# Token scales moved from x to the projections, and x laid out transposed, in a hybrid attention and Hyena encoder layer on one Trainium2 core

## The chip, the cores and the metric

The kernel runs on one core of one Trainium2 chip, as one launch. The metric is the device time in microseconds; the time before is the median of three runs, 1343.47 us (1342.41 to 1346.18). The profile below is of one further execution, of 1344.2 us from its first to its last instruction. Engines are named as in the profile: PE does matmuls (PEld: its weight loads), DVE, ACT and POOL do elementwise work, SP issues most transfers.

## What is computed

One encoder layer is applied to two sequences of 512 tokens by 1024 channels, all in float32. The layer norms x, projects it, sends a third of the projected columns each way through dilated attention (q, k, v) and Hyena (u), and ends with an output projection and an MLP. What the change touches is the beginning:

```
def rmsnorm(x, g):
    y = x * rsqrt(mean(x * x, axis=-1) + EPS) * g
...
xn = rmsnorm(x, mix_norm)
proj = xn @ w_in                      # 1024 -> 512 q, 512 k, 512 v, 1536 u
q = rope(rmsnorm_f32(q, q_norm))      # per head of 64
k = rope(rmsnorm_f32(k, k_norm))
attn = dilated_attention(q, k, v)
hy = hyena_mixer(u, ...)              # width-3 conv along tokens, then two gated long convolutions
h = x + concat(rmsnorm(attn), rmsnorm(hy)) @ w_out
y = h + square(relu(rmsnorm(h) @ w_up)) @ w_down
```

The norm of x has one factor for each token and one for each channel. The projection sums over channels, so the token's factor can be applied before it or after it.

## The kernel before

Every float32 product is formed of three matmuls on operands split in a high and a low part (mm3, line 75): high by high, high by low, low by high. Operands are named so: xh and xl are x normed, transposed to [channel, token] and split, one pair of tiles for each sequence with eight blocks of 128 channels; whi and wlo are weights; ih and il, yh and yl are inputs of the transforms.

**Ahead of the projections.** x is loaded as [token, channel], four tiles of 128 tokens for each sequence (load_x, line 138). norm_x (line 161) sums the squares of each tile (half on DVE, half on ACT), takes the power -1/2 on POOL, scales the tile in place (x<-x,ssx), and then, channel block by channel block, turns the four tiles on PE into a bank (pst<-ident,x, line 178), from which ACT makes xh with the channel's gain and DVE makes xl. The gains come as rows of a parameter tile that PE turns into columns (line 151). norm_x of the first sequence runs before all else; that of the second is a stream among others.

**The projections.** proj_u (line 372) does quarter q of u: for each sequence and each of three parts a, 24 matmuls of 128x512 into a bank psu of two; ACT and DVE then form the width-3 convolution y from the bank (one ACT pass, two DVE passes), PE turns y (pst<-ident,y), ACT copies it out as ut, and SP stores it (u_d). proj_qkv forms q, k and v in banks psq of two, 48 matmuls of 128x256 each; for q and k the sum of squares of each head goes through DVE and POOL to a power, and rotary tables ab, made on POOL by rope_tables, are multiplied in; v is copied out by one ACT pass of a bank.

**Beside them.** The Hyena filters (hidden, filters) and then the Hyena units (hyena(q, o), for four quarters and two orders) run transforms: psf forward, psi inverse, each of four classes of 12 matmuls. A class runs psf, then products on DVE (t), a split (yh, yl), then psi. Behind the last projection come the attention and the output projection; the MLP follows as further phases.

**What sets the order.** The work up to the MLP is written as generators, which interleave (line 489) calls by turns: each yields what PE and DVE time it believes it has emitted, and the stream whose work should be ready, by priority, goes next. The streams are: norm_x of the second sequence, then tables, hidden, filters of the four quarters; two streams of Hyena units that begin when the filters are done; one stream of U0 to U3, the Q projections and the attention; and the output projection. What is written this way is then scheduled when the program is built, and each engine executes its list in order: an instruction that waits holds all behind it on that engine. Transfers wait in the same way on SP's queue.

Of the kernel before, what the change touches and what calls it, by code (L numbers as in the profile page):

```python
# [24 lines left out]
# ring sizes  # L25
# [30 lines left out]
def hybrid_encoder_kernel(ctx: ExitStack, tc: tile.TileContext, i: dict, outs, dbg=None):  # L56
# [8 lines left out]
    # ---------------------------------------------------------------- helpers  # L65
# [9 lines left out]
    def mm3(ps, pairs, start=True, stop=True):  # L75
        """ps += sum of products of split operands (w_hi, w_lo, x_hi, x_lo)."""
        n = 3 * len(pairs)
        k = 0
        for wh, wl, xh, xl in pairs:
            for w, x in ((wh, xh), (wh, xl), (wl, xh)):  # L80
                nc.tensor.matmul(ps, lhsT=w, rhs=x, start=start and k == 0, stop=stop and k == n - 1)  # L81
                k += 1
# [24 lines left out]
    ssx = cp.tile([128, 8], F32, name="ssx")  # L107
    ssh = cp.tile([128, 8, 4], F32, name="ssh")
# [3 lines left out]
    # banks of the attention, while the hyena's are in use  # L112
# [3 lines left out]
    def rstd(out, ss, n):  # L116
        """out = (ss / n + eps) ** -0.5 for a few columns."""
# [4 lines left out]
    # ================================================================ phase A  # L122
# [13 lines left out]
    xs = {}  # L136

    def load_x(s, queue=nc.sync, pin=lambda x: x):
        for t in range(4):
            if s == 0 or t == 0:  # L140
                xs[s, t] = rz.tile([128, D], F32, name="x", tag="z", bufs=ZB)
            else:
                xs[s, t] = re_.tile([128, D], F32, name="x", tag="g", bufs=3)
            pin(queue.dma_start(xs[s, t], x_in[s][t * 128:(t + 1) * 128]))
# [4 lines left out]
    nc.sync.dma_start(i2, i["c_i2"])  # L149
    ps0 = bank("ps0", "tr")  # L150
    nc.tensor.transpose(ps0[:, :128], prm, ident)
    nc.vector.tensor_copy(cols, ps0[:, :80])
# [8 lines left out]
    def norm_x(s):  # L161
        for t in range(4):
            x = xs[s, t]
            c = slice(4 * s + t, 4 * s + t + 1)
            junk = [lw.tile([128, 512], F32, name="junk", tag=("y", "ut")[k], bufs=2) for k in range(2)]
            lo, hi = x[:, :512], x[:, 512:]
            nc.vector.tensor_tensor_reduce(out=junk[0], in0=lo, in1=lo, scale=1.0, scalar=0.0,
                                           op0=ALU.mult, op1=ALU.add, accum_out=rsc[:, 0, c])
            act(junk[1], hi, AF.Square, accum_out=rsc[:, 1, c])
            tt(nc.vector, ssx[:, c], rsc[:, 0, c], rsc[:, 1, c], ALU.add)  # L170
            rstd(ssx[:, c], ssx[:, c], D)
            act(hi, hi, AF.Copy, scale=ssx[:, c])
            nc.vector.tensor_scalar(lo, lo, ssx[:, c], None, op0=ALU.mult)
            yield 0, 1.2, 0
        for d in range(8):
            ps = bank("pst", "hx")
            for t in range(4):
                nc.tensor.transpose(ps[:, t * 128:(t + 1) * 128], xs[s, t][:, d * 128:(d + 1) * 128], ident)
# [1238 lines left out]
```

## Time and profile before

| | |
|---|---|
| median of three runs | 1343.47 us (1342.41 to 1346.18) |
| the profiled execution, its span | 1344.2 us |
| instructions | 19082 |
| POOL | busy 145.1 us, 11% of the span, 121 instructions |
| DMA | 184.46 MB, mean 137 GB/s |

The span in 40 equal slices of 33.6 us, each digit the busy share of a slice in tenths; PEclk is the clock granted to PE:

```
PE   6999999999999999999999999999999999999998
DVE  6887658888887755656557998788776688678885
ACT  6434424664565564557547643433333654334350
PEclk9999999999999989999999999999999999999999
```

Slice 1 holds the loading and scaling of x; slices 2 to 6 the u projections and filters; slices 7 to 13 the Q projections and Hyena units; slices 14 to 20 the attention and the output projection; the rest is the MLP. PE is the engine that fills the span, so the time is PE's matmuls plus what PE waits, plus what it loses at a lower clock. An instruction of the profile is given as line, engine, operation, output<-inputs; a wait is put down to the engine and tile that released it.

### The profile page before, as it was taken

What the parts mean: (1) busy time and instruction counts of PE and PEld (TensorE: products, weight loads), DVE (VectorE), ACT (ScalarE), POOL (GpSimd) and SP (SyncE); (2) the same over time, 40 slices, a digit from 0 to 9 for tenths busy, and PEclk for the clock granted to TensorE, in tenths of its full rate; (3) what the DMA queues carried; (4) which work ended last, traced back from release to release, by engine and by line L of the source; (5) the groups of instructions that cost most, each with busy time, mean ns of one, the idle gap of its engine ahead of it and who ended that gap; (6) DMA issues with size and microseconds to landing.
All of it is one profiled execution on the core that took longest, in us unless ns stands there. A gap on an engine that the chain in (4) does not pass through costs nothing.

```text
span 1344.2 us, 19082 instructions
## 1 busy us (share of the span) xinstructions
PE 1312.8 (98%) x6933; PEld 1097.1 (82%) x6933; DVE 1000.6 (74%) x1579; ACT 647.2 (48%) x1463; POOL 145.1 (11%) x121
## 2 busy tenths in 40 slices
PE   6999999999999999999999999999999999999998
PEld 5788889999999767776787788888887888887887
DVE  6887658888887755656558997788776688678885
ACT  6434424664565564557547643433333654334350
POOL 1100001343343030021004000000000000001000
PEclk9999999999999989999999999999999999999999
DMA  7535324224331573232141454544428753463323
GB/s 248 188 114 165 120 93 135 78 67 139 113 92 49 149 241 107 88 112 102 48 135 38 157 189 140 162 152 154 142 104 313 279 167 126 157 235 109 94 64 125
DMA packets 137235, 184.46 MB, mean 137 GB/s; under 512 B 9580, under 2 KB 77076, under 8 KB 137141
## 3 DMA queue, kind: packets, MB, share of 16 engines
q1 hardware_dynamic: 135700, 176.70, 40.7%
q0 software_dynamic: 864, 4.46, 0.9%
q10 hardware_dynamic: 576, 2.10, 0.4%
q8 instruction: 54, 0.88, 0.3%
q14 instruction: 41, 0.33, 0.1%
HBM read 122.66 MB, written 60.56 MB: 136 GB/s over the span
## 4 chain that ended last, share of the span: by engine, by line
PE 85%; DVE 8%; ACT 3%; DMA 2%; issue 2%; POOL 1%; SPq 0%; DVEq 0%; ACTq 0%
PE pu L81 24%; PE pn L81 19%; PE psu L81 10%; PE psq L81 6%; PE psw L81 6%; PE psf L81 4%; PE pss L81 4%; PE psi L81 3%; PE psp L813 2%; PE pv L820 1%; PE pv L819 1%; DVE clo L70 1%; PE po L832 1%; PE pst L372 1%; DVE t L70 1%
## 5 line engine op out<-in xcount | busy, mean ns | idle before, releaser
L81 PE MATMUL pu<-hn,chl 128*128 128x512 f32 x768 | 184.9, 390 | 1.9 <-POOL hn L70 1.9
L81 PEld LDWEIGHTS pu<-hn,chl 128*128 128x128 f32 x768 | 144.1, 188 | 32.4 <-POOL hn L70 2.7
L81 PE MATMUL pn<-hn,chl 128*128 128x512 f32 x576 | 141.5, 392 | 2.0 <-ACT chl L67 1.7
L81 PEld LDWEIGHTS pn<-hn,chl 128*128 128x128 f32 x576 | 108.7, 189 | 26.1 <-ACT chl L67 2.6
L67 ACT ACTIVATE chi<-fa 128x1024 fp32r<-128x1024 f32 x49 | 51.9, 1060 | 124.5 <-PE pu L81 63.1
L81 PE MATMUL psq<-wlo,xh 128*128 128x256 f32 x384 | 108.8, 283 | 0.4 <-DVE wlo L70 0.4
L81 PE MATMUL psq<-whi,xl 128*128 128x256 f32 x384 | 108.7, 283 | 0.0
L81 PE MATMUL psq<-whi,xh 128*128 128x256 f32 x384 | 108.6, 283 | 0.0
L70 DVE TENSOR_TENSOR clo<-fa,chi 128x1024 fp32r<-128x1024 f32 x49 | 61.3, 1251 | 39.4 <-ACT chi L67 39.4
L81 PE MATMUL pu<-chi 128*128 128x512 f32 x248 | 86.5, 397 | 2.0 <-DVE chi L70 1.1
L81 PE MATMUL pu<-clo,chi 128*128 128x512 f32 x200 | 78.2, 391 | 1.6 <-DVE clo L70 1.6
L81 PE MATMUL pn<-chi 128*128 128x512 f32 x228 | 79.1, 389 | 0.0
L67 ACT ACTIVATE chl<-tmp 128x512 fp32r<-128x512 f32 x64 | 40.3, 631 | 79.7 <-PE pu L81 49.1
L81 PE MATMUL psu<-xh,whi 128*128 128x512 f32 x192 | 77.9, 409 | 0.5 <-ACT xh L67 0.5
L81 PE MATMUL pu<-chi,clo 128*128 128x512 f32 x200 | 77.8, 389 | 0.0
L81 PE MATMUL psu<-xl,whi 128*128 128x512 f32 x192 | 76.9, 401 | 0.0
L81 PE MATMUL psf<-ih,dft 128*128 128x256 f32 x384 | 76.7, 283 | 0.0
L81 PE MATMUL psu<-xh,wlo 128*128 128x512 f32 x192 | 76.2, 398 | 0.0
L81 PE MATMUL pn<-clo,chi 128*128 128x512 f32 x192 | 74.9, 390 | 0.1
L81 PE MATMUL pn<-chi,clo 128*128 128x512 f32 x192 | 74.7, 389 | 0.0
L81 PEld LDWEIGHTS psq<-wlo,xh 128*128 128x128 f32 x384 | 73.7, 192 | 0.6 <-DVE wlo L70 0.6
L81 PEld LDWEIGHTS psq<-whi,xh 128*128 128x128 f32 x384 | 73.7, 192 | 0.0
(246 smaller groups left out, 3240.1 us busy)
## 6 DMA issues: line engine op xcount, KB each, us to landing
fa<-f_d SPq DMA_DIRECT2D x49, 512.0 KB, 3.7
wur<-in_w_up_t_dram SPq DMA_DIRECT2D x32, 512.0 KB, 4.2
f_d<-x SPq DMA_DIRECT2D x60, 256.0 KB, 2.8
wd<-in_w_down_dram SPq DMA_DIRECT2D x14, 1024.0 KB, 7.7
f_d<-s SPq DMA_DIRECT2D x45, 256.0 KB, 2.1
wraw<-in_w_u_dram SPq DMA_DIRECT2D x24, 256.0 KB, 2.9
u_d<-ut SPq DMA_DIRECT2D x24, 256.0 KB, 2.5
z<-u_d SPq DMA_DIRECT2D x24, 256.0 KB, 4.1
```

What stands on the lines that cost most here:

```text
L67: nc.scalar.activation(out, in_, func, **kw)
L70: eng.tensor_tensor(out, a, b, op=op)
L81: nc.tensor.matmul(ps, lhsT=w, rhs=x, start=start and k == 0, stop=stop and k == n - 1)
L372: nc.tensor.transpose(pt[:, t], y[:, t * 128:(t + 1) * 128], ident)
L813: nc.tensor.transpose(ps[:, t * 128:(t + 1) * 128], exps[n][1 + t][:, kt * 128:(kt + 1) * 128], ident)
L819: nc.tensor.matmul(pv, lhsT=w, rhs=ph, start=kt == 0, stop=False)
L820: nc.tensor.matmul(pv, lhsT=w, rhs=pl, start=False, stop=kt == 3)
L832: nc.tensor.matmul(po[:, t], lhsT=ot[:, t * 128:(t + 1) * 128], rhs=i2, start=True, stop=True)
```

## The change

The host lays x out a second time, as [sequence, pair of channel blocks, channel, block, token], and the parameters as columns, so that neither is turned on PE. xh and xl are then made from the loaded block directly, with the channel's gain and without the token's factor. The squares of a block are summed over blocks by ACT and POOL; PE sums them over channels by products with a column of ones and spreads the resulting factors over the partitions by four plain f32 products with the identity (token_scales); ACT copies them out as the tile scales.

The token's factor is applied behind the projections: to u's bank by one DVE product before the convolution; to v by ACT's copy, now one for each half bank; for q and k, whose heads are normed anyway, only the epsilon changes (epsx), by two operations in place of one. The copy of x that is added to the output is loaded as before.

The first pass, that of the first quarter of u for the first sequence, is written block by block: each channel block goes into three banks at once as it arrives, and the three banks wait for the scales. The rotary tables share their memory with scales and are made behind the last u projection. In the diff, blank lines and comments are left out:

```diff
-    nc.sync.dma_start(ident, i["c_ident"])
...
-    prm = re_.tile([128, 128], F32, name="prm", tag="t", bufs=TB)
-    nc.sync.dma_start(prm, i["params"])
-    load_x(0)
-    nc.tensor.transpose(ps0[:, :128], prm, ident)
-    nc.vector.tensor_copy(cols, ps0[:, :80])
+    pin(nc.sync.dma_start(cols, i["params"]))
...
+    scales = lw.tile([128, NSEQ, 512], F32, name="scales", tag="ab")
+    def load_x(s, j):
+        if s == 0 or j == 0:
+            xr[s, j] = rz.tile([128, 2, 512], F32, name="x", tag="z", bufs=ZB)
+        else:
+            xr[s, j] = re_.tile([128, 2, 512], F32, name="x", tag="g", bufs=3)
+        pin(nc.sync.dma_start(xr[s, j], i["x_t"][s, j]))
+    def prep_x(s, d):
+        x = xr[s, d // 2][:, d % 2]
+        act(xh[s][:, d], x, AF.Copy, scale=col(R_MIX + d))
+        stt(xl[s][:, d], x, col(R_MIX + d), f32(xh[s][:, d]), ALU.mult, ALU.subtract)
+        sq = re_.tile([128, 512], F32, name="sqx", tag="t", bufs=TB)
+        act(sq, x, AF.Square)
+        if d == 0:
+            ssum[s] = sq
+        else:
+            tt(nc.gpsimd, ssum[s], ssum[s], sq, ALU.add)
+    def token_scales(s):
+        c = slice(4 * s, 4 * s + 4)
+        ps = bank("pst", "hx", [128, 4])
+        for t in range(4):
+            nc.tensor.matmul(ps[:, t:t + 1], lhsT=ssum[s][:, t * 128:(t + 1) * 128], rhs=one, start=True, stop=True)
+        marks = [nc.vector.tensor_scalar(rsc[:, 0, c], ps, 1.0 / D, EPS, op0=ALU.mult, op1=ALU.add),
+                 nc.gpsimd.tensor_tensor(ssx[:, c], rsc[:, 0, c], mhalf[:, :4], op=ALU.pow)]
+        nc.vector.tensor_scalar(epsx[:, c], rsc[:, 0, c], EPS, None, op0=ALU.mult)
+        ps = bank("pst", "hx")
+        for t in range(4):
+            nc.tensor.matmul(ps[:, t * 128:(t + 1) * 128], lhsT=ssx[:, 4 * s + t:4 * s + t + 1].to_broadcast([128, 128]),
+                             rhs=ident, start=True, stop=True)
+        return [m.ins for m in (*marks, nc.scalar.activation(scales[:, s], ps, AF.Copy))]
+    def norm_x(s, marks):
         for d in range(8):
-            ps = bank("pst", "hx")
-            for t in range(4):
-                nc.tensor.transpose(ps[:, t * 128:(t + 1) * 128], xs[s, t][:, d * 128:(d + 1) * 128], ident)
-            act(xh[s][:, d], ps, AF.Copy, scale=col(R_MIX + d))
-            stt(xl[s][:, d], ps, col(R_MIX + d), f32(xh[s][:, d]), ALU.mult, ALU.subtract)
-            yield 0.43, 0.66, 0
+            with tc.issue_after(marks[0]), tc.issue_after(marks[1]), tc.issue_after(marks[2]):
+                prep_x(s, d)
+            yield 0, 0.8, 0
+        token_scales(s)
+        yield 1.2, 1.2, 1.0
...
     def proj_u(q, w=None, begun=()):
...
+                if s == 0 and begun:
+                    ps = begun[a]
+                    if a > 1:
+                        turn(*todo.pop(0))
+                        yield 0.43, 0, 0
...
+                tt(nc.vector, ps, ps, scales[:, s], ALU.mult)
                 y = lw.tile([128, 512], F32, name="y", tag="y", bufs=2)
                 act(y, ps, AF.Identity, scale=col(R_CW + 12 + ch), bias=col(R_CB + ch))
...
             if which == 2:
-                act(o, ps)
+                for a in range(2):
+                    act(o[:, a], ps[:, a], AF.Copy, scale=ssx[:, 2 * mp + a:2 * mp + a + 1])
...
-            rstd(rr, rr, HD)
+            for a in range(2):
+                nc.vector.tensor_scalar(rr[:, 4 * a:4 * a + 4], rr[:, 4 * a:4 * a + 4], 1.0 / HD,
+                                        epsx[:, 2 * mp + a:2 * mp + a + 1], op0=ALU.mult, op1=ALU.add)
+            tt(nc.gpsimd, rr, rr, mhalf[:, :8], ALU.pow)
...
-    w0 = load_w(w_u[0], first=True)
+    w_raw = []
+    for j in range(4):
+        load_x(0, j)
+        for k in ((0, 1), (2,), (3, 4), (5,))[j]:
+            w_raw.append(lw.tile([128, 512], F32, name="wraw", tag="wraw", bufs=4) if k < 4 else
+                         re_.tile([128, 512], F32, name="wraw", tag="t", bufs=TB))
+            pin(nc.sync.dma_start(w_raw[k], w_u[0][:, k]))
+    pin(nc.sync.dma_start(ident, i["c_ident"]))
+    for j in range(4):
+        load_x(1, j)
+    w0, begun = [], [bank("psu", tag) for tag in ("mm", "mm", "hx")]
+    for j in range(4):
+        prep_x(0, 2 * j)
+        w0 += load_w(w_u[0], ((0, 1), (2,), (3, 4), (5,))[j], first=True)
+        prep_x(0, 2 * j + 1)
+        for e in (2 * j, 2 * j + 1):
+            for a in range(3):
+                mm3(begun[a], [(*u_unit(w0, e, a), xh[0][:, e], xl[0][:, e])], start=e == 0, stop=e == 7)
+    marks = token_scales(0)
...
-        rope_tables()
...
-        stream(("x1", (), norm_x(1)), ("t", (), tables()), ("h", (), hidden()), ("F0", (), filter0()),
+        stream(("x1", (), norm_x(1, marks)), ("t", (), tables()), ("h", (), hidden()), ("F0", (), filter0()),
...
-        stream(*[(f"U{q}", (), proj_u(q, w0 if q == 0 else None)) for q in range(4)],
+        stream(*[(f"U{q}", (), proj_u(q, *((w0, begun) if q == 0 else ()))) for q in range(4)],
+               ("T", (), rope_tables()),
```

Three places show how the engines' lists change. The first is PE's list at the end of the first pass, in before the last transposes of x (pst<-ident,x) of the first 72 psu matmuls; xh_117 and xl_119 belong to the first sequence there, and so do xh_106 and xl_108 in the changed kernel, where xh_107 and xl_109 are the second's:

```order
51 L178 MATMUL pst<-ident,x 128x128 x4
52 L81 MATMUL psu<-xh_117,wlo 128x512
53 L178 MATMUL pst<-ident,x 128x128 x8
54 L372 MATMUL pst<-ident,y 128x128 x4
55 L81 MATMUL psu<-xh_117,whi 128x512
56 L81 MATMUL psu<-xl_119,whi 128x512
```

```order
64 L81 MATMUL psu<-xl_108,whi 128x512
65 L81 MATMUL psu<-xh_106,wlo 128x512
66 L173 MATMUL pst<-one,sqx 128x1 x4
67 L179 MATMUL pst<-ident,ssx 128x128 x4
68 L386 MATMUL pst<-ident,y 128x128 x4
69 L81 MATMUL psu<-xh_107,whi 128x512
```

The transposes of x are gone. In their place all 72 matmuls of the first pass stand ahead of the sums over channels (row 66), the spreading of the scales (67) and the turning of the first y (68), and no matmul of the second sequence stands before row 69.

The second place is DVE's list at the same point. In before, the first y stands among the second sequence's xl:

```order
46 L70 TENSOR_TENSOR ssx<-rsc 128x1 x2
47 L119 TENSOR_SCALAR ssx<-ssx 128x1 x2
48 L173 TENSOR_SCALAR x<-x,ssx 128x512 x2
49 L73 SCALAR_TENSOR_TENSOR y<-psu,cols,y 128x511 x3
50 L73 SCALAR_TENSOR_TENSOR xl_120<-pst,cols,xh_118 128x512
51 L73 SCALAR_TENSOR_TENSOR y<-psu,cols,y 128x511
52 L73 SCALAR_TENSOR_TENSOR xl_120<-pst,cols,xh_118 128x512 x7
```

```order
10 L70 TENSOR_TENSOR wlo<-wraw,whi 128x512
11 L174 TENSOR_SCALAR rsc<-pst 128x4
12 L176 TENSOR_SCALAR epsx<-rsc 128x4
13 L70 TENSOR_TENSOR psu<-psu,scales 128x512 x3
14 L73 SCALAR_TENSOR_TENSOR xl_109<-x,cols,xh_107 128x512 x8
15 L73 SCALAR_TENSOR_TENSOR y<-psu,cols,y 128x511 x6
```

Now the three banks are scaled first, then all eight xl of the second sequence are made, and only then the first y. ACT's list has the same order: the copy of the scales, then eight xh and six squares of the second sequence, then the first y. The first entry of ACT's list, its table load, which waits for nothing in before, now carries the wait for the first block of x.

The third place is ACT's list at the end of the projections, from the copies of v's last banks (qo<-psq) on; ih and yh are the splits of a Hyena class ahead of its psf and of its psi, v<-vin is the attention's reload of v:

```order
251 L67 ACTIVATE ih<-sd 128x512
252 L67 ACTIVATE ih<-craw 128x512 x2
253 L67 ACTIVATE qo<-psq 128x512
254 L67 ACTIVATE yh<-t_4593 128x512
255 L67 ACTIVATE wsb<-psi 128x512
256 L67 ACTIVATE qo<-psq 128x512
257 L67 ACTIVATE yh<-t_4698 128x512
258 L67 ACTIVATE yh<-t_4839 128x512
259 L67 ACTIVATE wsb<-psi 128x512
260 L67 ACTIVATE qkh<-psk 128x512 x2
261 L67 ACTIVATE v_5461<-vin 128x8x64
262 L67 ACTIVATE yh<-t_4900 128x512
```

```order
251 L67 ACTIVATE qo<-psq,ssx 128x256 x2
252 L67 ACTIVATE ih<-sd 128x512 x2
253 L67 ACTIVATE ih<-craw 128x512
254 L67 ACTIVATE v_5431<-vin 128x8x64
255 L67 ACTIVATE ih<-craw 128x512
256 L67 ACTIVATE yh<-t_4465 128x512
257 L67 ACTIVATE v_5440<-vin 128x8x64
258 L67 ACTIVATE qkh<-psk 128x512 x2
259 L67 ACTIVATE wsb<-psi 128x512
260 L67 ACTIVATE qkh<-psk 128x512 x2
261 L67 ACT_TABLE_LOAD
262 L67 ACTIVATE pe,den<-pe,mx 128x512
```

Behind the last copy of v stood three yh of the last Hyena unit; now all four ih of it stand there too, with the reload of v ahead of the last one.

More of the change, by code (lines that the diff above doesn't have):

```diff
@@ L102, in hybrid_encoder_kernel @@
     ident = cp.tile([128, 128], F32, name="ident")
-    nc.sync.dma_start(ident, i["c_ident"])
+    one = cp.tile([128, 1], F32, name="one")
+    nc.vector.memset(one, 1.0)
     mhalf = cp.tile([128, 16], F32, name="mhalf")
@@ L107, in hybrid_encoder_kernel @@
     ssx = cp.tile([128, 8], F32, name="ssx")
+    epsx = cp.tile([128, 8], F32, name="epsx")
     ssh = cp.tile([128, 8, 4], F32, name="ssh")
@@ L159, in hybrid_encoder_kernel @@
     xl = [la.tile([128, 8, S], F32R, name=f"xl{s}") for s in range(NSEQ)]
-    def norm_x(s):
-        for t in range(4):
[L163 to L174, printed above, removed]
-        for d in range(8):
-            ps = bank("pst", "hx")
-            for t in range(4):
-                nc.tensor.transpose(ps[:, t * 128:(t + 1) * 128], xs[s, t][:, d * 128:(d + 1) * 128], ident)
-            act(xh[s][:, d], ps, AF.Copy, scale=col(R_MIX + d))
-            stt(xl[s][:, d], ps, col(R_MIX + d), f32(xh[s][:, d]), ALU.mult, ALU.subtract)
-            if s == 0 and d == 3:
-                load_x(1, nc.scalar, tc.keep_in_program_order)
-            yield 0.43, 0.66, 0
@@ L191, in load_w @@
             lo = lw.tile([128, 512], F32R, name="wlo", tag="wlo", bufs=WB)
-            raw = (re_.tile([128, 512], F32, name="wraw", tag="t", bufs=TB) if first and k > 1 else
-                   lw.tile([128, 512], F32, name="wraw", tag="wraw", bufs=4))
-            nc.sync.dma_start(raw, src[:, k])
+            if first:
+                raw = w_raw[k]
+            else:
+                raw = lw.tile([128, 512], F32, name="wraw", tag="wraw", bufs=4)
+                nc.sync.dma_start(raw, src[:, k])
@@ L385, in proj_u @@
                 ch = 4 * a + q
-                ps = bank("psu", "mm")
-                for d in range(0, 8, 2):
-                    mm3(ps, [(*unit(e, a), xh[s][:, e], xl[s][:, e]) for e in (d, d + 1)], start=d == 0, stop=d == 6)
-                    yield 1.28, 0, 0
-                    if d == 2 and todo:
-                        turn(*todo.pop())
-                        yield 0.43, 0, 0
+                if s == 0 and begun:
+                    ps = begun[a]
+                    if a > 1:
+                        turn(*todo.pop(0))
+                        yield 0.43, 0, 0
+                else:
+                    ps = bank("psu", "mm")
+                    for d in range(0, 8, 2):
+                        mm3(ps, [(*u_unit(w, e, a), xh[s][:, e], xl[s][:, e]) for e in (d, d + 1)], start=d == 0, stop=d == 6)
+                        yield 1.28, 0, 0
+                        if d == 2:
+                            while todo:
+                                turn(*todo.pop(0))
+                                yield 0.43, 0, 0
+                tt(nc.vector, ps, ps, scales[:, s], ALU.mult)
                 y = lw.tile([128, 512], F32, name="y", tag="y", bufs=2)
@@ L507, in interleave @@
                 break
+    ab = None
     def rope_tables():
+        nonlocal ab
+        ab = lw.tile([128, 4, 4, 64], F32, name="ab", tag="ab")
         cs = lw.tile([128, 4, 2, 32], F32, name="cs", tag="y", bufs=2)
@@ L594, in filter0 @@
         yield from filters(0)
-    for _ in norm_x(0):
-        pass
     done.add("x0")
```

38 lines of the change are left out of this document (17 added, 21 removed).

## The prediction

> **What bounds the kernel now.** The profiled execution lasted 1344.2 us from its first to its last instruction; the median of the three timed runs is 1343.47 us. I make the sum against 1344.2 and read the result as a median, since the two differ by less than 0.1%. First the table of engines, then the waits of PE (columns: us in total, times, longest):
>
> ```profile
> PE 1312.8 (98%) x6933; PEld 1097.1 (82%) x6933; DVE 1000.6 (74%) x1579; ACT 647.2 (48%) x1463; POOL 145.1 (11%) x121
> ...
> PE pst L178 <- DVE x L173: 6.6, 4, 4.3
> ```
>
> PE is busy 98% of the span, and its longest wait by total, 6.6 of the 31.4 us that are left, is for x to be scaled in the first 15 us. So only three things can move the end: matmuls that go or come, the first microseconds, and new idle time of PE. Now the timeline of PE (start, length), and its totals in some stretches (length, then busy us and count, granted clock behind them):
>
> ```profile
> 15.29 1.22 PE L81 MATMUL psu<-xh,whi 128*128 128x512 f32 x2 [0.51 <-ACT xh L67]
> ...
> 18.01 0.63 PE L81 MATMUL psu<-xh,whi 128*128 128x512 f32 x1
> 18.44 0.63 PE L81 MATMUL psu<-xl,whi 128*128 128x512 f32 x1
> ...
> 21.42 0.39 PE L81 MATMUL psu<-xl,whi 128*128 128x512 f32 x1
> 21.65 0.40 PE L81 MATMUL psu<-xh,wlo 128*128 128x512 f32 x1
> ...
> 39.67 1.04 PE L178 MATMUL pst<-ident,x 128*128 128x128 f32 x8
> ...
> 41.01 0.48 PE L81 MATMUL psu<-xl,whi 128*128 128x512 f32 x1
> ...
> 15.29:41.01 25.72, 20.54 (x70) 13.90 (x71) 2.90 (x4) 1.56 (x2) 1.00 0.75 270
> ...
> 475.00:480.00 5.00, 2.87 (x21) 1.00 1.06 339
> 480.00:482.00 2.00, 1.17 (x9) 1.00 1.06 373
> ...
> 482.20:492.40 10.20, 10.20 (x33) 0.50 0.74 258
> ...
> 738.00:741.60 3.60, 1.60 (x5) 1.00 0.00 0
> 741.60:745.00 3.40, 3.40 (x9) 0.50 0.15 11
> ```
>
> Projection work starts at 15.29. A 128x512 matmul follows the last after 0.43 us until 21.4 us and after 0.23 us from then on: half clock for 6.1 us. By 41.01 us, 70 of the first sequence's 72 are done (the row 15.29:41.01 counts psu alone; PEld and the other engines follow PE in it), and all 64 transposes of x lie before that point, 0.11 us each at full clock (eight in 1.04 with the last one's tail), with two turned y. The other rows show what a pause costs: 2.96 us of idle PE between 475 and 482 us, then half clock to about 492 us though PE is busy throughout; 2.0 us of idle before 741.6, then half clock for 3.4 us.
>
> **The change, part by part.** *The first pass starts earlier.* Rows of ACT and SP:
>
> ```profile
> 0.72 1.28 ACT L67 ACT_TABLE_LOAD   x1 [0.72 <-PEq L1406]
> 1.64 1.86 SPq L144 DMA_DIRECT2D x<-in_x_prompt_dram  x4
> 5.48 0.63 ACT L67 ACTIVATE junk<-x 128x512 f32<-128x512 f32 x1 [3.47 <-DMA x<-in_x_prompt_dram]
> 6.82 0.63 ACT L67 ACTIVATE junk<-x 128x512 f32<-128x512 f32 x1 [0.62 <-DMA x<-in_x_prompt_dram]
> ...
> 11.88 1.13 ACT L67 ACTIVATE whi<-wraw 128x512 fp32r<-128x512 f32 x2
> 28.15 1.34 ACT L67 ACTIVATE x<-x,ssx 128x512 f32<-128x512 f32 x2 [1.39 <-POOL ssx L70]
> ```
>
> The first block of x is now second on SP's queue, not third, so it lands about 0.5 us earlier, at 5.0. ACT's table load, which ran at 0.72 us under cover, now holds the wait for that block: 1.28 us more, 6.3. Two xh (0.67 each, as x<-x,ssx) and a whi (0.57): first matmul at 8.2, against 15.29. The rest of x and w (3.0 MB) lands by 13, at 1.34 us for 512 KB (5.48 to 6.82). ACT's 8 xh, 6 whi and 8 squares take 8 x 0.67 + 14 x 0.57 = 13.3 us, to 19.6, well ahead of PE. With 6.1 us at half clock as before (14 matmuls) and 58 x 0.23 = 13.3, the 72 end at 27.6.
>
> *But then PE waits.* By the order, it next forms the sums of squares, spreads the scales, and turns the first y before the second sequence's first matmul:
>
> ```profile
> L70 POOL TENSOR_TENSOR rsc<-rsc,mhalf 128x4 f32<-128x4 f32 x2 | 2.0, 1006 | 85.6 <-DVE rsc L119 85.6
> ...
> L230 PE MATMUL psh<-ft,wr 33*128 33x512 f32 x4 | 2.2, 641 | 0.0
> L70 DVE TENSOR_TENSOR t<-psf,hs 128x512 f32<-128x512 f32 x64 | 40.7, 682 | 8.5 <-PE psf L81 5.1 <-issue 2.1 <-POOL il L70 1.2
> L67 ACT ACTIVATE ut<-pst 128x512 f32<-128x512 f32 x24 | 14.2, 593 | 4.9 <-PE pst L372 4.7
> L67 ACT ACTIVATE y<-psu,cols 128x512 f32<-128x512 f32 x24 | 18.7, 778 | 62.3 <-PE psu L81 55.8 <-POOL ab L70 6.5
> L119 DVE TENSOR_SCALAR rr<-rr 128x8 f32<-128x8 f32 x16 | 2.7, 170 | 8.2 <-ACT sq L67 8.2
> ...
> 31.71 2.19 DVE L73 SCALAR_TENSOR_TENSOR y<-psu,cols,y 128x511 f32<-128x511 f32 x3 [2.51 <-ACT y L67]
> 33.39 0.63 PE L372 MATMUL pst<-ident,y 128*128 128x128 f32 x4 [0.41 <-DVE y L73]
> ```
>
> Plain f32 products occur in before at 512 columns, four records in 2.2 us for two: 1.1 each, so 0.27 for 128 columns; a single column is bounded by 0 and 0.27, and I take 0.2, as its weights still have to be loaded. The wait: 0.8 (four single columns), 0.17 (DVE), 1.0 (POOL's power of 128x4), 1.1 (four spreads), 0.6 (ACT's copy): scales at 31.3. Only then does ACT take up the second sequence, and its 8 xh and 6 squares stand ahead of the first y: 8 x 0.67 + 6 x 0.57 = 8.8, then 0.8 for y and three DVE passes of 0.73: 43.1. DVE's scaling of the three banks (as t<-psf,hs, a product of a bank and a tile: 0.68 each) and its eight xl run beside ACT. With the turn (0.63) the second sequence starts at 43.7. Before, two matmuls were missing at 41.01: 41.5. That is 2.2 us late, and one turn (4 x 0.11) is still owed: **+2.6**. PE has then been idle for 12 us in one piece, so it restarts at half clock. By the rows above that lasts 3.4 to 10.2 us and costs 0.47 us for each (0.43 against 0.23 a matmul): 1.6 to 4.8. I take 5.1 us, between the 3.4 and the start's 6.1: **+2.4**. The second sequence's scales cost PE 0.8 + 1.1 = **+1.9**, their wait covered by projections. In all **+7**; with a denser start and a short ramp it is +3, with a long one +10.
>
> The Trainium skill, in "TensorE: Matmul & The Clock Gate", section "Why this matters for your kernels", speaks against the change here: a pause of more than about 3 us between bursts of matmuls puts the clock back to half. The trace agrees, and shows it for 2.0 us of idle too (738 to 741.6). By the page's Part 1 one busy window of about 3.4 us lifts the clock again, which would make my 2.4 an estimated 1.6; the trace at 482 to 492 shows three times that, 4.8.
>
> *Scaling in the banks.* 24 DVE passes of 0.68 = 16 us come into a stretch that PE bounds and DVE nearly fills:
>
> ```profile
> 40.00:50.00 10.00, 10.00 (x47) 6.78 (x45) 8.36 (x12) 3.40 (x7) 5.22 (x10) 1.00 0.40 113
> 50.00:60.00 10.00, 10.00 (x45) 7.41 (x44) 9.13 (x16) 6.12 (x10) 0.00 (x0) 1.00 0.32 91
> 60.00:80.00 20.00, 20.00 (x92) 15.81 (x91) 18.02 (x35) 7.95 (x13) 0.00 (x0) 1.00 0.54 158
> ```
>
> Behind the length stand PE, PEld, DVE, ACT and POOL: DVE is busy 9.13 of 10 and 18.02 of 20. Three or four more passes in 20 us put it over 100%. PE has projections of later quarters to go on with, so I price the direct wait at 0 to 4, **+2**. What suffers is the filters, which slide behind the projections. The second tensor_scalar per bank of q and k (0.17 on DVE) and v's second copy (at most the 0.59 of ut on ACT) come where these engines have slack. The rotary tables now stand behind the last U; POOL's ten operations are the 5.2 us in the fifth place of 40 to 50. Against them stands PE's rate late among the Q matmuls:
>
> ```profile
> 430.00:440.00 10.00, 10.00 (x86) 1.00 0.09 28
> ```
>
> 86 matmuls in 10.0 us, 0.12 each: two banks of Q (96 matmuls, 11.5 us) hide the 5.2; uncovered they would cost all of it.
>
> *The far end of the projections.* Before the first Q matmul PE's order holds 240 psf matmuls in before and 192 now; behind the last one it holds 12 psf and 36 psi in before, 48 and 48 now: a whole Hyena unit of four classes instead of the end of one. Rows of that place (first and last start), and of the engines that feed a class:
>
> ```profile
> L81 PE MATMUL psq<-whi,xl x38: 279/283/283, 424.8 to 443.9; 128*128 128x256 f32 x38
> ...
> L81 PE MATMUL psi<-yh,dft x31: 279/283/562, 440.4 to 458.1; 128*128 128x256 f32 x31
> ...
> 440.00:460.00 20.00, 17.59 (x111) 0.91 0.77 193
> 460.00:480.00 20.00, 16.93 (x81) 1.00 0.64 190
> ...
> L70 DVE TENSOR_TENSOR t<-t,t 128x256 f32<-128x256 f32 x64 | 32.1, 548 | 0.2
> L70 DVE TENSOR_TENSOR yl<-t,yh 128x512 fp32r<-128x512 f32 x32 | 26.5, 839 | 5.8 <-ACT yh L67 5.5
> L67 ACT ACTIVATE yh<-t 128x512 fp32r<-128x512 f32 x32 | 20.2, 632 | 17.0 <-DVE t L70 16.2 <-DVE rr L119 0.7
> ```
>
> The 48 left over took 14.2 us (443.9 to 458.1) in a stretch where PE was idle 2.4 of 20 us and lost a tenth of its clock. The order puts 36 psf and 12 psi more there. A class runs in turn: 12 matmuls (1.4), four DVE passes (2 x 0.68 + 2 x 0.55), yh 0.63, yl 0.84, 12 matmuls (1.4): 6.7 us. Three more with nothing beside them: 20; less the 5.8 us that PE works on 48 matmuls, 14 of idle and half clock; if attention's first heads fill it all, 0. Since PE was already idle there before, and ACT's order puts the reload of v ahead of a class's split, I take the upper end less a little: **+13**.
>
> Sum: 1344.2 + 7 + 2 + 13 = 1366.
>
> **The rivals.** *Only the start costs* (1348 to 1354): attention fills the tail. For it: PE finds work everywhere between 60 and 430 us. Against it: the idle time of 440 to 480 us. 1344.2 + 7 + 0 = 1351. *A deep tail* (1375 to 1390): the pauses there bring three more half-clock stretches like that of 482 to 492 (4.8 each), and the rotary tables stand open: 1366 + 14.4 + 5.2 = 1386. *Break-even* (within 0.3%, about what a measurement of this kernel tells from no change): the start costs 3, tail 0: 1347. *Faster*, the other side: the start pays. PE begins 7.1 us earlier; if the pause at 27.6 us were short, that would be kept. The length of the pause decides. With y straight behind the scales it is 16.1 - 8.8 = 7.3 us in place of my 16.1 (27.6 to 43.7), and with the short ramp the start gives 3 - 8.8 = -6: 1338, the tail filled. Above some 13 us of pause nothing is won. ACT's order, with 14 operations ahead of y, speaks against it.
>
> **How the numbers follow.** The forecast (1354 to 1375) 0.52, start alone 0.18, deep tail 0.16, break-even 0.09, faster 0.05. Slower by over 0.3%: 0.52 + 0.18 + 0.16 = 0.86; within: 0.09; faster: 0.05. The range 1348 to 1384 leaves out the last two and a third of the deep tail, 0.19.
>
> **What would show it.** The first psu matmul near 8 us, the 72nd near 27.6; a PE wait of 10 us or more before pst<-ident,y; granted clock 0.50 behind it; the second sequence from about 43.7; filters (psf) some 20 us later than before; between the last psq and the last psi at least 25 us, with PE busy under 85%; the last stages unchanged in length. Wrong would be: no wait at y, or a Hyena tail that PE fills.

## The result, and the profile after

The changed kernel takes 1389.03 us (median of four runs, 1385.06 to 1390.32) against 1343.05 for the kernel before: a ratio of 1.034, 95% interval 1.0319 to 1.0361, or 46 us more (the kernel before now as the median of four runs). The profiled execution spans 1386.8 us, 42.6 more than the 1344.2 of before. First the table of engines and two rows of the span in 40 slices (here 34.7 us each), then the waits of PE (us in total, times, longest):

```profile
PE 1319.0 (95%) x6900; PEld 1099.0 (79%) x6900; DVE 1022.3 (74%) x1583; ACT 647.7 (47%) x1465; POOL 169.6 (12%) x129
...
PE   6599999999999779999998999999999999999998
PEclk9799999999999889999999999999999999999999
```

```profile
PE pst L386 <- DVE y L73: 18.1, 4, 17.1
PE psu L81 <- ACT whi L67: 8.6, 1, 8.6
PE psf L81 <- ACT ih L67: 7.2, 6, 2.1
PE psi L81 <- ACT yh L67: 6.0, 2, 3.6
```

PE has 33 matmul records fewer (65 for the transposes of x and the parameters are gone, 32 for sums and spreads have come, two for each plain f32 product) and is busy 6 us longer, in part because more of them run at half clock. Two places are dark: slices 1 and 2, the second of them in clock too, and slices 14 and 15 in both. The start, from PE's timeline and those of the engines that it waits for:

```profile
8.56 0.80 PE L81 MATMUL psu<-xh,whi 128*128 128x512 f32 x1 [8.56 <-ACT whi L67]
...
27.51 0.39 PE L81 MATMUL psu<-xh,wlo 128*128 128x512 f32 x1
27.73 0.95 PE L173 MATMUL pst<-one,sqx 128*128 128x1 f32 x8
30.04 1.74 PE L179 MATMUL pst<-ident,ssx 128*128 128x128 f32 x8 [1.36 <-POOL ssx L175]
48.83 1.09 PE L386 MATMUL pst<-ident,y 128*128 128x128 f32 x4 [17.05 <-DVE y L73]
49.57 0.78 PE L81 MATMUL psu<-xh,whi 128*128 128x512 f32 x1
...
53.98 0.56 PE L81 MATMUL psu<-xl,whi 128*128 128x512 f32 x1
54.38 0.40 PE L81 MATMUL psu<-xh,wlo 128*128 128x512 f32 x1
```

```profile
7.40 1.41 DVE L73 SCALAR_TENSOR_TENSOR xl<-x,cols,xh 128x512 fp32r<-128x512 f32 x2 [6.50 <-ACT xh L67]
8.73 1.28 DVE L70 TENSOR_TENSOR wlo<-wraw,whi 128x512 fp32r<-128x512 f32 x2
...
13.59 1.78 DVE L70 TENSOR_TENSOR wlo<-wraw,whi 128x512 fp32r<-128x512 f32 x1
...
32.45 1.89 DVE L70 TENSOR_TENSOR psu<-psu,scales 128x512 f32<-128x512 f32 x3 [3.37 <-ACT scales L181]
34.25 12.46 DVE L73 SCALAR_TENSOR_TENSOR xl<-x,cols,xh 128x512 fp32r<-128x512 f32 x8
46.63 2.71 DVE L73 SCALAR_TENSOR_TENSOR y<-psu,cols,y 128x511 f32<-128x511 f32 x4
```

```profile
34.75 11.41 POOL L70 TENSOR_TENSOR sqx<-sqx 128x512 f32<-128x512 f32 x7 [4.76 <-ACT sqx L67]
```

```profile
40.33 1.43 ACT L67 ACTIVATE y<-psu,cols 128x512 f32<-128x512 f32 x2
```

The first pass ends at 27.9 us; after the sums and the spreads PE stands for 17.05 us in one piece, restarts at half clock at 48.83, and is at full clock from 54.4. ACT has its first y at 41.1, but DVE, in order, does all eight xl ahead of the passes of y. With POOL's additions beside it one xl takes 1.56 us (12.46 for eight); the two at 7.40, without them, take 0.70 each.

Behind that, the windows (busy us and count of PE, PEld, DVE, ACT, POOL; then the clock, the DMA share and GB/s) in the filter stretch, one of before and then those of after, the last three behind the last projection; and the rows of psq and psi (duration in ns, shortest, median and longest, then first and last start):

```profile
120.00:140.00 20.00, 20.00 (x118) 17.36 (x117) 11.98 (x20) 8.11 (x14) 0.00 (x0) 1.00 0.34 105
```

```profile
120.00:140.00 20.00, 18.11 (x88) 14.97 (x87) 14.07 (x24) 7.35 (x13) 0.00 (x0) 0.91 0.37 122
...
240.00:260.00 20.00, 17.63 (x131) 17.03 (x130) 15.57 (x27) 8.38 (x46) 10.37 (x14) 0.91 0.35 101
...
460.00:480.00 20.00, 13.68 (x75) 11.63 (x74) 13.94 (x21) 7.16 (x13) 2.79 (x2) 0.83 0.62 168
480.00:500.00 20.00, 15.93 (x81) 11.90 (x80) 14.00 (x35) 10.73 (x23) 0.48 (x1) 0.91 0.09 26
500.00:520.00 20.00, 13.53 (x54) 9.61 (x54) 10.19 (x22) 13.37 (x40) 11.64 (x11) 0.79 0.79 258
```

```profile
L81 PE MATMUL psq<-whi,xl x384: 277/283/420, 235.6 to 460.7; 128*128 128x256 f32 x192
```

```profile
L81 PE MATMUL psi<-yh,dft x256: 274/282/415, 254.4 to 498.4; 128*128 128x256 f32 x128
```

From the last psq to the last psi there are 37.7 us (14.2 before), in which (460 to 500) PE is idle for a good quarter and loses a tenth to a sixth of its clock. To see what each stage adds, I take **PE's loss**: the time at which PE has reached a point of its work, less the sum of all matmuls ahead of that point at the spacing that they have in before at full clock (0.227 us for 128x512, 0.118 for 128x256). Worked out from the start times of the trace for points at 40, 240, 400, 540, 680 and 1000 us of work, in us for each stretch:

| PE's loss in | before | after | more |
|---|---|---|---|
| the first 40 us of work (to 58.6 and 73.5 us on the clock) | 18.5 | 33.3 | 14.8 |
| 40 to 240: u projections beside filters | 5.7 | 16.6 | 10.9 |
| 240 to 400: Q projections beside Hyena units | 2.5 | 1.9 | -0.6 |
| 400 to 540: end of the projections, first half of attention | 23.1 | 32.4 | 9.3 |
| 540 to 680: attention, output projection | 16.4 | 21.3 | 4.9 |
| 680 to 1000: first MLP product | -2.2 | 3.3 | 5.5 |
| the rest | -2.3 | -2.0 | 0.3 |

The last column sums to 45.1; PE's work itself is 2.5 us less; that makes the 42.6. The first two columns depend on the spacings put in (most 128x256 matmuls of the trace start 0.120 apart, and the smaller shapes have no single spacing), which is why some entries are negative. With other spacings the last column moves by up to some 2 us a stretch, so it is the one to read, and each kernel stands for one execution.

### The profile page after: what moved, and what is told of

The parts are those of the page before. It is cut to its first block, busy times and chain, and to the rows that moved or that the text cites. A ratio compares the mean times of both kernels' runs of the same rounds, so it can differ in the third digit from the quotient of the medians.

```text
span 1386.8 us, 19057 instructions
## 1 busy us (share of the span) xinstructions
PE 1319.0 (95%) x6900; PEld 1099.0 (79%) x6900; DVE 1022.3 (74%) x1583; ACT 647.7 (47%) x1465; POOL 169.6 (12%) x129
## 4 chain that ended last, share of the span: by engine, by line
PE 60%; DVE 4%; ACT 2%; DMA 2%; issue 1%; POOL 0%; SPq 0%; DVEq 0%; ACTq 0%
PE pu L81 23%; PE pn L81 18%; PE psw L81 5%; PE pss L81 3%; PE psq L81 2%; PE psp L857 2%; PE psi L81 1%; PE pv L864 1%; PE po L876 1%; PE pv L863 1%; DVE clo L70 1%; PE psf L81 1%; DMA tmp<-f_d 1%; DMA hyr<-hy_d 1%; POOL hn L70 0%
## 5 line engine op out<-in xcount | busy, mean ns | idle before, releaser
L81 PE MATMUL pu<-hn,chl 128*128 128x512 f32 x768 | 187.7, 394 | 1.7 <-POOL hn L70 1.7
L67 ACT ACTIVATE chi<-fa 128x1024 fp32r<-128x1024 f32 x49 | 51.9, 1059 | 124.8 <-PE pu L81 63.1
L81 PE MATMUL psf<-ih,dft 128*128 128x256 f32 x384 | 80.1, 290 | 7.2 <-ACT ih L67 7.2
```

The lines of the kernel that those rows point to most:

```text
L67: nc.scalar.activation(out, in_, func, **kw)
```

## The experiments

All results, as medians, and as ratios to the kernel before run beside them. The last columns are counted in the program's order: psu matmuls ahead of the first psf, psf ahead of the first psq, and psf and psi behind the last psq.

| kernel | us | ratio (95% interval) | psu | psf | behind |
|---|---|---|---|---|---|
| before | 1343 | 1 | 264 | 240 | 12 + 36 |
| after | 1389.0 | 1.0340 (1.0319 to 1.0361) | 312 | 192 | 48 + 48 |
| e1 filters late | 1357.3 | 1.0118 (1.0090 to 1.0145) | 288 | 180 | 60 + 72 |
| e2 preparation free | 1373.6 | 1.0233 (1.0210 to 1.0256) | 288 | 240 | 24 + 48 |
| e3 the same, sums on DVE | 1359.8 | 1.0123 (1.0105 to 1.0140) | 240 | 240 | 24 + 48 |
| e4 18 of 24 scalings out | 1369.4 | 1.0194 (1.0179 to 1.0209) | 308 | 194 | 48 + 48 |
| e5 after, 64 bytes more | 1386.6 | 1.0327 (1.0303 to 1.0351) | 312 | 192 | 48 + 48 |
| e6 before, 64 bytes more | 1348.2 | 1.0039 (1.0023 to 1.0054) | 264 | 240 | 12 + 36 |
| e7 before, products by ones | 1349.4 | 1.0053 (1.0036 to 1.0071) | 264 | 241 | 12 + 36 |
| e8 start repaired | 1360.6 | 1.0137 (1.0106 to 1.0168) | 264 | 240 | 24 + 48 |
| e9 after, addresses of before | 1383.3 | 1.0302 (1.0281 to 1.0324) | 312 | 192 | 48 + 48 |
| e10 repaired, addresses of before | 1351.3 | 1.0084 (1.0051 to 1.0117) | 264 | 240 | 24 + 48 |
| e11 ones, addresses of before | 1345.2 | 1.0028 (1.0012 to 1.0045) | 264 | 241 | 12 + 36 |
| e12 ones and filters late | 1359.8 | 1.0140 (1.0113 to 1.0167) | 288 | 180 | 60 + 72 |
| e13 e10, 18 scalings out | 1347.0 | 1.0037 (1.0022 to 1.0052) | 264 | 240 | 24 + 48 |
| e14 e10, filters late by 8 | 1356.6 | 1.0110 (1.0093 to 1.0127) | 288 | 192 | 48 + 48 |
| e15 e9, sums on DVE | 1376.5 | 1.0244 (1.0215 to 1.0273) | 312 | 192 | 48 + 48 |
| e16 e10, filters late by 12 | 1361.8 | 1.0140 (1.0102 to 1.0178) | 312 | 192 | 48 + 48 |
| e17 e16, 18 scalings out | 1355.4 | 1.0101 (1.0074 to 1.0129) | 336 | 192 | 46 + 48 |

**The filters' place alone (e1).** The kernel before, with one line:

```diff
     def hidden():
+        yield 0, 0, 15.4
         ft = re_.tile([33, 1024], F32, name="ft", tag="dec")
```

> The kernel before with one edit: the stream of the filter work is held back by 15.4 us, the length of the first pass, which the changed kernel no longer has among the interleaved work. Start, scaling in banks and layout are those of before. Theory A (the first pass taken out of the interleaving lets the filters start with less projection work left to cover them, so more of the Hyena units stand behind the last projection): start unchanged, 60 psf and 72 psi matmuls behind the last psq in place of 12 and 36, PE idle and at half clock there, 1355 to 1365 us against 1343 of before. Rival B (the loss is made in the first 60 us, and the rest only moves): within 1340 to 1348.

Theory A held: 13 us slower by the medians, 16 by the ratio, with the start as before. Its windows behind the last projection look like those of the changed kernel:

```profile
460.00:480.00 20.00, 14.27 (x49) 10.10 (x48) 13.86 (x30) 7.50 (x28) 1.69 (x2) 0.64 0.10 27
480.00:500.00 20.00, 16.51 (x61) 11.86 (x61) 8.51 (x19) 13.68 (x40) 11.61 (x9) 0.67 0.92 298
```

PE works 30.8 of 40 us there, at two thirds of its clock. Its loss from 400 to 540 us of work is 33.0, 9.9 more than before; from 40 to 240 only 2.3 are added.

**The preparation's place (e2), and who adds the squares (e3).**

```diff
         for d in range(8):
-            with tc.issue_after(marks[0]), tc.issue_after(marks[1]), tc.issue_after(marks[2]):
-                prep_x(s, d)
+            prep_x(s, d)
```

and in e3 also

```diff
-            tt(nc.gpsimd, ssum[s], ssum[s], sq, ALU.add)
+            tt(nc.vector, ssum[s], ssum[s], sq, ALU.add)
```

> The changed kernel without the rule that issues the second sequence's preparation behind the first one's scales on ACT, DVE and POOL. Theory A (that preparation, standing ahead of the first y on ACT and DVE, makes the 17.1 us pause and the half clock behind it): the wait before the first y falls to 3 to 7 us, the second sequence starts at 35 to 39 us in place of 49.6, 1368 to 1378 us in place of 1389. Rival B (the scales' own chain of five steps makes the pause): the wait stays over 10 us and the time above 1384.

> As the run before it, with the sums of squares over the channel blocks added on DVE and no longer on POOL. Theory A (DVE's xl and wlo run at half speed while POOL adds beside them, 1.56 against 0.70 us for one xl): xl and wlo at 0.64 to 0.75 us throughout the first 40 us, the second sequence from 32 to 36 us, 1360 to 1370 us. Rival B (xl is slow for another reason, or DVE isn't what the start waits for): xl stays near 1.5 us, or the time equals that of the run before within 3 us or is above it, as DVE has 14 more additions.

e2 gave the time of theory A, but not its start. The waits of PE from 20 to 60 us:

```profile
PE pst L179 <- POOL ssx L175: 7.1, 1, 7.1
PE pst L385 <- DVE rsc L174: 2.3, 1, 2.3
```

The first y is no longer waited for. Now the scales come late, since DVE has the eight xl ahead of the first operation on them, still slowed by POOL; the second sequence starts at 42.8 us, not at 35 to 39. The whole group of xl and that of the additions, in the view by line, first in the changed kernel and then in e3:

```profile
L70 POOL TENSOR_TENSOR sqx<-sqx 128x512 f32<-128x512 f32 x14 | 21.9, 1568 | 15.4 <-ACT sqx L67 14.5
L73 DVE SCALAR_TENSOR_TENSOR xl<-x,cols,xh 128x512 fp32r<-128x512 f32 x16 | 21.7, 1410 | 7.2 <-ACT xh L67 7.2
```

```profile
L73 DVE SCALAR_TENSOR_TENSOR xl<-x,cols,xh 128x512 fp32r<-128x512 f32 x16 | 11.5, 744 | 6.1 <-ACT xh L67 6.1
L70 DVE TENSOR_TENSOR sqx<-sqx 128x512 f32<-128x512 f32 x14 | 9.6, 685 | 0.6 <-DVE epsx L176 0.4
```

The 16 xl took DVE 21.7 us beside POOL's 14 additions and take 11.5 without: 10 us, and the additions cost DVE 9.6 us when it does them itself. e3 is 14 us faster than e2, at the lower edge of theory A; 48 fewer psu matmuls stand ahead of its first psf, so not all of that need be DVE's. Its second sequence starts at 42.2 us, again later than I said, in part because PE now does 3.8 us of the filters' first layer ahead of it.

**POOL's additions alone (e15).** The edit of e3 without that of e2, at the addresses of before (below):

> The changed kernel at the addresses of before (1383.3 us), with the sums of squares on DVE, and the second sequence's preparation still behind the scales. Theory (eight xl at 0.75 and seven additions at 0.69 are 10.8 us of DVE, against 12.5 for eight xl at 1.56): xl at 0.70 to 0.75 us, the pause before the first y 15 to 16.5 us in place of 17.1, 1379 to 1384 us: the place of the preparation and not POOL's additions makes the pause. Rival (POOL's additions make most of it): pause below 12 us, 1365 to 1375 us.

PE's wait for y in e15:

```profile
PE pst L386 <- DVE y L73: 14.6, 4, 13.6
```

Between the two forecasts: an xl takes 0.70 us again, the pause falls by 3.5 us, to 13.6, and the time by 7. That is more than the theory's sum, since the scheduler now puts passes of y ahead of the last two additions. 13.6 us of pause stay without POOL's additions, while e2 and e3 have no wait for y at all: the place of the preparation makes most of the pause, POOL some 3.5 us of it.

**The products in the banks (e4, e7, e11, e12).** In e4 `if q == 0:` stands ahead of the scaling in proj_u. In e7 the kernel before gets

```diff
+                tt(nc.vector, ps, ps, onesx[:, :1].to_broadcast([128, 512]), ALU.mult)
                 y = lw.tile([128, 512], F32, name="y", tag="y", bufs=2)
```

with `onesx` a new tile of 128 bytes; in e11 the ones stand in an unused column of mhalf; e12 is e11 with the line of e1.

> The changed kernel with the multiplication of u's banks by the token scales left out in quarters 1 to 3 (18 of 24; those columns of u stay unscaled). Theory A (the start and the filters' lateness make most of the loss, the scaling itself a few us in the filter stretch from 100 to 230 us): 1377 to 1386 us, and PE's loss of time up to 60 us as in the changed kernel. Rival B (the DVE passes in the banks are what fills DVE and so delays the filters and everything behind them): 1350 to 1370 us.

> The kernel before with one DVE product more for each of the 24 banks of u, by ones, in the place where the changed kernel applies the token scales; no other edit. Theory A (DVE is nearly full in the stretch from 40 to 220 us, so 16 us more work there put off the filters and Hyena units, which end as idle and half-clocked PE behind the last projection): 8 to 18 us more, 1351 to 1361. Rival B (the projections hide it, as the prediction priced it): 0 to 4 us more, below 1347.5.

> The kernel before with the 24 products by ones in u's banks, and all addresses as in before, where the run with ones in a tile of its own had them shifted by 128 bytes. Theory (of the 7 us of that run about 5 were the shift): 1342 to 1347 us, so the pass itself costs 0 to 4 where the rest is as before, which was the prediction's price. Rival (the pass costs 7): 1348 to 1352 us.

> The kernel before with both the filters held back by 15.4 us and the 24 products by ones, addresses as in before. Theory (the two work on the same reserve: with the filters late there is nothing left to hide the DVE passes, which is why 18 of them cost 20 us in the changed kernel and next to nothing in before): more than the sum of the two, 1343 + 13.4 + 10 or more, 1364 to 1378 us. Rival (they add up, and the changed kernel's sensitivity comes from its start): 1356 to 1361 us.

In the changed kernel 18 products are worth 20 us, which was rival B's forecast (1369.4), and PE's loss from 40 to 240 us of work falls from 16.6 to 7.7; in before all 24 cost 3.8 us (e11), which was the prediction's price. Filters late and products together (e12) cost 18.8, and apart 15.9 and 3.8: in the whole time they add up, as the rival said. In the stretch from 40 to 240 us of work they don't: PE's loss there is some 2 us above before's in e1 and in e11, and some 6 in e12. e7 fell between its two forecasts; it has e11's products and a shift of addresses by 128 bytes, which by the next runs is worth 5 us, and is 3 us slower than e11.

**Addresses (e5, e6, e9).** A tile of 64 bytes a partition is added in e5 and e6; in e9 the new tiles vanish into old ones:

```diff
-    one = cp.tile([128, 1], F32, name="one")
+    one = mhalf[:, 15:16]
...
-    epsx = cp.tile([128, 8], F32, name="epsx")
+    epsx = rsc[:, 3]
```

> The changed kernel with 64 bytes of padding behind its new small tiles, so that every tile on the left side of the memory stands 128 bytes behind its place in before, and no longer 64. The instructions are the same. Theory (in the first MLP product a matmul follows the last after 231.1 ns in all four profiles of kernels with the new tiles, and after 226.7 ns in both without them; there the operands stand at different places within 128 bytes): 226.7 ns again, 1344 x 4.4 ns = 6 us less and a little more in the output projection, 1381 to 1384 us. Rival (the slower rate has another cause, as the history of the clock): 231 ns as before, the time within 2 us of 1389.

> The kernel before with 64 bytes of padding at the same place, and nothing else. Theory (place within 128 bytes): 231 ns for a matmul of the first MLP product, 1348 to 1351 us. Rival: 226.7 ns and within 2 us of before.

> The changed kernel with its two new small tiles (the column of ones and the epsilons) kept in unused parts of tiles that before has too, so that every tile on the left side stands at the address that it has in before. Shifts by 64 and by 128 bytes both gave 230.5 to 231.1 ns for a matmul of the first MLP product, so place within 128 bytes is not what decides. Theory (the distance between the operands on the left and on the right side of the memory decides): 226.7 ns again, 4 to 6 us less than 1389, 1381 to 1385. Rival (something else of the changed kernel): 230 to 231 ns, 1386 to 1390.

The same group of 768 matmuls, by line, in before, after, e6 (before, shifted by 64 bytes), e5 (after, shifted by 128 in all) and e9 (after, not shifted); behind the count stand busy us and mean ns:

```profile
L81 PE MATMUL pu<-hn,chl 128*128 128x512 f32 x768 | 184.9, 390 | 1.9 <-POOL hn L70 1.9
```

```profile
L81 PE MATMUL pu<-hn,chl 128*128 128x512 f32 x768 | 187.7, 394 | 1.7 <-POOL hn L70 1.7
```

```profile
L81 PE MATMUL pu<-hn,chl 128*128 128x512 f32 x768 | 187.8, 394 | 1.8 <-POOL hn L70 1.8
```

```profile
L81 PE MATMUL pu<-hn,chl 128*128 128x512 f32 x768 | 187.3, 393 | 1.8 <-POOL hn L70 1.8
```

```profile
L81 PE MATMUL pu<-hn,chl 128*128 128x512 f32 x768 | 185.2, 391 | 2.0 <-POOL hn L70 2.0
```

e5's theory fell, e6's and e9's held. From start to start, in the middle of the first MLP product, one matmul follows another after 226.7 ns in before and e9, 231.1 in after and e6, and 230.6 in e5 and e7. In before all starts are 226 or 227 ns apart; in e6 the distances repeat every twelve matmuls, from 224 to 236 ns. Half of the moving tiles (hn) there lie on the left side and shift with the small tiles, while the weights (chl) lie on the right and don't. 1344 x 4.4 ns = 5.9 us; by e9, 0.0038 of 1343 = 5.1 us, give or take 4.

**The repaired start (e8, e10).** The edits of e2 and e3, and

```diff
-                    ps = bank("psu", "mm")
+                    ps = bank("psu", "hx" if q == 0 and s == 1 and a == 0 else "mm")
```

with the tile of e5 (e8) or the edit of e9 (e10).

> The changed kernel with the second sequence's preparation free to start at once, the sums of squares on DVE, the padding of 64 bytes, and the second sequence's first bank taken from another set of banks, so that it doesn't wait for the first y. Theory (the start, the padding and the pass in the banks are all of the loss): by what the runs showed 1359.8 - 6 - 3 to 8 for the rest of the pause, 1346 to 1351 us. Rival (the projections now run into the same limit of DVE, and the gain is given back in the filters and the tail): 1352 to 1358 us.

> The changed kernel with the preparation free, the sums on DVE, the second sequence's first bank apart, as in the repaired start before, and the addresses of before. Theory (addresses are worth 4 to 6 us): 1353 to 1357 us. Rival: 1359 to 1362 as with the shift of 128 bytes.

e8 came out above both of its forecasts, and no faster than e3 (1.0137 against 1.0123): the bank of its own brought nothing that shows. e10's median lies 2 us below its theory's range, its ratio (1354 us) inside it; the rival fell. Neither e10 nor any other version reaches the kernel before.

**The order in the repaired kernel (e13, e14, e16, e17).** e14 and e16 are e10 with `yield 0, 0, 8` and `yield 0, 0, 12` at the place of e1; e13 and e17 leave out the scaling as e4 does, from e10 and e16.

> The kernel with the repaired start and the addresses of before (1351.3 us), with the multiplication of u's banks left out in quarters 1 to 3 (18 of 24; those columns stay unscaled). Theory A (the passes are dear only where the late start has used up DVE's reserve): 1347 to 1352 us. Rival B (they cost by themselves what they cost in the changed kernel): 1330 to 1338 us.

> The kernel with the repaired start and the addresses of before, with the filter stream held back by 8 us, which gives it the changed kernel's numbers: 192 psf ahead of the first psq, 48 psf and 48 psi behind the last. Theory A (the order carries much of the 32 us that the repaired start gave): 1362 to 1370 us, the loss between 430 and 530 us. Rival B (the order is nearly neutral, and the pause with what it does to DVE carries them): 1350 to 1357 us.

> The kernel with the repaired start and the addresses of before (1351.3 us), its filter stream held back by 12 us, which gives it 312 psu ahead of the first psf, 192 psf ahead of the first psq, and 48 psf and 48 psi behind the last: the changed kernel's numbers. Theory A (with fewer projections left beside the filters PE meets their chains with nothing else to do, so the order carries the rest): 1363 to 1372 us, 8 us or more of it lost between 90 and 250 us. Rival B (the pause itself, and what it puts off on DVE, carries it): 1354 to 1360 us.

> The repaired kernel with the filter stream held back by 12 us (1361.8), with the multiplication of u's banks left out in quarters 1 to 3 (18 of 24; those columns stay unscaled). Theory A (where the filters stand late, DVE's passes in the banks come between their chains and PE, so the products are dear there): 10 us or more less, 1343 to 1352 us, and the loss between 90 and 250 us back to that of the repaired kernel. Rival B (it takes the pause as well): 3 to 6 us less, 1356 to 1359 us.

The first window of the filter stretch in e10, e14, e16 and e17:

```profile
80.00:120.00 40.00, 40.00 (x209) 32.36 (x209) 31.24 (x53) 14.61 (x25) 0.00 (x0) 1.00 0.52 156
```

```profile
80.00:120.00 40.00, 37.67 (x173) 30.36 (x172) 31.49 (x55) 14.57 (x25) 0.00 (x0) 0.91 0.45 130
```

```profile
80.00:120.00 40.00, 38.90 (x186) 31.15 (x185) 32.17 (x56) 14.60 (x25) 0.00 (x0) 0.96 0.47 133
```

```profile
80.00:120.00 40.00, 40.00 (x203) 33.11 (x201) 31.31 (x55) 16.73 (x28) 0.00 (x0) 1.00 0.51 149
```

With the filters late, PE runs dry between 80 and 120 us and its clock drops: its loss from 40 to 240 us of work is 5.4 in e10, 15.7 in e14 and 13.2 in e16 (16.6 in the changed kernel). But e17, whose filters stand as late as e16's and which lacks 18 products, keeps PE full and at full clock there, and its loss is back within some 2 us of before's, as its theory A said. So two things make that stretch's loss together: above before's 5.7 it is 0 to 3 us with the products alone (e10, e11) or with the lateness and few or no products (e1, e4, e17), and 6 to 11 with both (e12, e14, e16, the changed kernel). That DVE's passes in the banks come between the late chains and PE is my reading of it.

Whole, the lateness costs 3.5 us in e14, as its rival B said, and 7.5 in e16 (0.0026 and 0.0056 of 1343), between the two; with the intervals of e10 and these, 5 and 7 us either way, e14's can't be told from no cost, and e16's barely. Part is given back later, as from 240 to 400 us of work, where e10 loses 4.9 and e14 1.3. The 18 products are worth 6.3 us in e10, where e13 met its theory A at the lower edge, and 5.2 in e16, where e17's time fell between its forecasts, close to rival B's; by the intervals each is good to 5 or 6 us. What makes them worth 20 in the changed kernel must lie in what e16 has not (the pause, POOL's additions, the shared bank, the shift of addresses); I haven't separated that further.

## Why the prediction was wrong

The direction and the main places were right, the sum of 1366 was 23 us short, and the range ended 5 us below the result. Step by step:

- **The first pass**: first matmul at 8.2 foretold, 8.56 measured; the 72nd ends at 27.9, not 27.6; scales copied by 32.4, not 31.3. Right within about 1 us.
- **The pause**: "DVE's scaling of the three banks (as t<-psf,hs, a product of a bank and a tile: 0.68 each) and its eight xl run beside ACT." This step failed. I followed ACT's order ahead of y and gave DVE's xl no time of their own. At 1.56 us each, with y's passes queued behind all eight, DVE ended last: 49.57 against 43.7 for the second sequence, 5.9 us, and a pause of 17.05 us where I had 12. At 0.70 each, by the sum, they would have ended near 40, ahead of ACT's first y; in e15 each takes 0.70, but DVE does the additions too, and the pause is 13.6. The half clock behind it and the second scales (0.8 and 1.0 us of PE) were right. In all the start cost 14.8 - 2.5 = 12.3 us (the 2.5 for the transposes that PE no longer does), where I put 7 and at most 10.
- **The clock**: 5.1 us of half clock foretold; it lasted 4.8 us from the second sequence's first matmul (49.57 to 54.38), 5.5 from the turn of y, within the 3.4 to 10.2 of before's rows. The Trainium skill's "TensorE: Matmul & The Clock Gate", Part 1, has one busy window of about 3.4 us end the half clock; here it took longer.
- **The filters' slide**: "PE has projections of later quarters to go on with, so I price the direct wait at 0 to 4". This step failed too. The scaling itself did cost that in the kernel before (e11: 3.8). But I had read off the order that the filters slide (the first psf starts at 124.8 us, not 98.3), and priced only what falls behind the last projection. Ahead of the first psf stand 312 of the 576 psu matmuls, not 264; 48 fewer are left to lie beside the filters' chains, with the products on DVE. PE lost 10.9 us more than in before between 40 and 240 us of work. e14 and e16 bring a like loss into the repaired kernel by the order, and e17, which has the order without 18 products, doesn't, nor does the changed kernel without them (e4): it takes the two together.
- **The far end**: +13 foretold; 9.3 from 400 to 540, and 4.9 in the stretch after it. The mechanism was right and the size close (14.2 for 13).
- **"The last stages unchanged in length"**: wrong by 5.5 us in the first MLP product, through addresses (e6, e9). The prediction put this term at nothing: the instructions there are the same, and it did not look at where the new small tiles move the operands.

The two rivals' sums of 1351 and 1338 leave out the 2 us for the scaling, on which nothing hangs. Of the rivals, *a deep tail* named a time near the result, for other reasons: the rotary tables were hidden but for 0.3 us of PE's wait, and the extra loss lies mostly ahead of the tail. *Faster* asked for the pause to be short; with the pause cut (e10) PE is at the second sequence at 39.1 us and still nothing is won: the scaling, the half clock and the units behind the last projection remain.

By ratios to before, the 46 us come apart so, each step with 4 to 7 us of uncertainty by the intervals, and with sizes that hold for this order of steps: addresses 5 (after to e9), POOL's sums 8 (e9 to e15), the preparation's place, together with the bank, 14 (e15 to e16, the same counts in the order), the filters' lateness 7.5 (e16 to e10), and 11 that stay in e10. Of those, 18 of the 24 products are 6 (e13), or all 24 in before 3.8; what is left fits the Hyena matmuls behind the last projection (24 + 48 for 12 + 36), which no run undoes alone.

## What to carry to other kernels

Ahead of an operation that PE waits for, count the queue of every engine in its chain, not only of the one that looks full, and price two-input operations on DVE at their speed beside POOL's work. When a piece of PE's work is taken out of an interleaved program, ask what it covered: the chains that ran beside it start with less left to hide them, and the loss shows where they run as well as at the end. Keep small new tiles from moving the addresses of operands, or compare with padded copies, when a per cent is at stake.

## What had not been expected of the hardware

DVE and POOL hold each other up: with POOL adding, an xl took 1.56 us, alone 0.70; a wlo 1.78 against 0.64. POOL's own addition took 1.60 beside the xl and 1.25 to 1.26 with DVE idle, in the last two of e2 (2.59 us with the gap between them); DVE does it in 0.68 (e15).

```profile
35.28 2.59 POOL L70 TENSOR_TENSOR sqx<-sqx 128x512 f32<-128x512 f32 x2
```

The Trainium skill bears on it: "GPSIMD Engine Reference", section "1. Specifications", names contention of POOL with DVE instructions that have two inputs in the SBUF, as xl and wlo have; the trace agrees.

A shift of 64 or 128 bytes of one side of the memory against the other lengthened the mean spacing of 1344 matmuls of 128x512 from 226.7 to 231.1 and 230.6 ns, with the same instructions. Which distance is good, and why, these runs don't show; the second MLP product, whose operands nearly all lie on the right side, kept 226.8 throughout.
